# Up projection of a ConvFFN: x's high and low parts side by side, 512 columns in one matmul

## The chip, the cores and the metric

The kernel runs on one core of one Trainium2 chip. The metric is the device time of one execution in microseconds: before the change the median of three timed runs is 317.19 us (317.07 to 317.27). The profile is of one further execution.

## The reference

The input x is 256 tokens of 1024 features in float32. One layer runs (DEPTH = 1), and it is of kind 0: attention in one block of 256 tokens, then a feed-forward part with a causal convolution over three tokens, then a last RMSNorm. Cut to what matters:

```python
hn = _rmsnorm(x, norm_mix[0])
x = x + _moba(hn, w_qkv, w_o)          # 16 heads of 64, plain causal attention at SEQ = 256
x = x + _conv_ffn(_rmsnorm(x, norm_ffn[0]), w_up, conv_w, conv_b, w_down)
return _rmsnorm(x, norm_final)

def _conv_ffn(x, w_up, conv_w, conv_b, w_down):
    u = _causal_dwconv(x @ w_up, conv_w, conv_b)      # 1024 -> 2 * 2816, width 3
    gate, up = jnp.split(u, 2, axis=-1)
    return (jax.nn.silu(gate) * up) @ w_down          # 2816 -> 1024
```

## The kernel before, in words

Precision comes from splitting. Every operand of a matmul is held as a high part (a copy rounded to the reduced float32 type F32R) and a low part (the rest). A product is then three matmuls: high by high, high by low, low by high; `mm3` (lines 227 to 231) writes all products but the first. TensorE takes the first operand of a matmul as the weights it holds, 128 x 128, and streams the columns of the second past them.

For weights, ScalarE makes the high part (`hi_cols`, line 176) and VectorE the low part (`lo_cols`, line 179), each in pieces of 1024 columns. The rows of the trace call such tiles whi and wlo, Vh and Vl, OTh and OTl (the attention's buffers, used again for weights), dhi and dlo (down weights).

x stands transposed, features on partitions: XTh and XTl, each 128 x 8 x 256, high and low part of the normed x without its factor per token. That factor is R (128 x 256, the same in each partition) and is multiplied in after the projection.

The feed-forward part is a loop over 22 chunks c of 128 hidden features (line 660). For each chunk:

- `up(c, 0)` and `up(c, 1)` project the gate half and the up half (g = 0 and 1): for each of 8 steps k over the features, `proj` issues the three matmuls of 128x256 into columns 0 to 255 of one PSUM bank. There are four such banks (psA), so chunk c + 2 takes those of chunk c.
- `scale_r` (line 618) is one VectorE product of the bank with R, into a padded tile (pad00 to pad11, two chunks by two halves).
- `center` (ScalarE, line 622) and two `conv` steps for each half (VectorE, line 627) do the convolution, `sact` (ScalarE, line 692) the silu, `m` (VectorE, line 697) the product of both halves. m is split into mh (ScalarE) and ml (VectorE).
- ScalarE and VectorE also split the down weights of this chunk and the up weights of chunk c + 3 in between.
- `down(c - 2)` adds chunk c - 2's part to the output: 12 matmuls of 128x512, six into the banks of psT and six into psS, which hold the sums over all chunks.

The order on each engine is that in which the code issues; each engine works through its own queue in order and waits by semaphores. Loads come through SyncE's queue as buffers come free. Chunks 0 and 1 are projected while the attention's last part still runs, chunks 2 to 21 in the loop, and chunk 21 has a shorter way of its own (`last_chain`). Behind the loop come the last down matmuls, the last norm and the stores.

Of the kernel before, what the change touches and what calls it, by code (L numbers as in the profile page):

```python
# [8 lines left out]
F32R = mybir.dt.float32r  # L9
BF16 = mybir.dt.bfloat16  # L10
AF = mybir.ActivationFunctionType
# [3 lines left out]
P = 128  # L15
S = 256
D = 1024
KT = D // P
NP = 8
DFF = 2816  # L20
NC = DFF // P
# [29 lines left out]
def hybrid_layer(ctx: ExitStack, tc: tile.TileContext, a):  # L51
    nc = tc.nc
    pe, dve, act, pool = nc.tensor, nc.vector, nc.scalar, nc.gpsimd

    cst = ctx.enter_context(tc.tile_pool(name="cst", bufs=1))
# [8 lines left out]
    def psA():  # L64
        return ps.tile([P, 512], F32, name="psA", tag="A", bufs=4)

    def psS(i):
        return ps.tile([P, 512], F32, name=f"psS{i}", tag=f"S{i}")
# [18 lines left out]
    pads = [[cst.tile([P, S + 2], F32, name=f"pad{i}{g}") for g in range(2)] for i in range(2)]  # L87
# [16 lines left out]
    first = head[:, NPRM:].rearrange("p (i k s) -> p i k s", i=3, k=KT)  # L104
    XTr = first[:, 0]
    x1 = XTr.rearrange("p (t k) s -> p t (k s)", t=2)
    XTh = cst.tile([P, KT, S], F32R, name="XTh")
    XTl = cst.tile([P, KT, S], F32R, name="XTl")
    R = cst.tile([P, S], F32, name="R")
    st = cst.tile([P, 32], F32, name="st")  # L110

# [97 lines left out]
    UP = [Unit(a["wup"][c], 2048, 2) for c in range(NC)]  # L209
# [17 lines left out]
    def mm3(out, l, r, first, last):  # L227
        (lh, ll), (rh, rl) = l, r
        pe.matmul(out, lh, rh, start=first, stop=False)  # L229
        pe.matmul(out, lh, rl, start=False, stop=False)  # L230
        pe.matmul(out, ll, rh, start=False, stop=last)  # L231
# [4 lines left out]
    def gain_lo(k, src, g):  # L236
        dve.scalar_tensor_tensor(XTl[:, k, :], src, g[:, k:k + 1], f32(XTh[:, k, :]),
                                 op0=ALU.mult, op1=ALU.subtract)

    def proj(out, unit, k, off):  # L240
        h, l = unit.v(unit.hi, KT), unit.v(unit.lo, KT)
        mm3(out[:, :S], (h[:, k, off:off + P], l[:, k, off:off + P]), (XTh[:, k, :], XTl[:, k, :]),
            k == 0, k == KT - 1)
# [9 lines left out]
    def bcast_R(c, alloc):  # L253

        rp = alloc()
        for t in range(2):
            pe.transpose(rp[:, t * P:(t + 1) * P], st[:, c + t:c + t + 1].to_broadcast([P, P]), ident)
        act.activation(R, rp[:, :S], AF.Copy)
# [106 lines left out]
    def v_mm(half, part, vp, ts=(0, 1)):  # L365
        u = VW[2 * half + part]
        h, l = u.v(u.hi, 4), u.v(u.lo, 4)
        for t in ts:
            for kk in range(4):
                k = 4 * part + kk  # L370
                tk = slice(t * P, (t + 1) * P)
                mm3(vp[t], (XTh[:, k, tk], XTl[:, k, tk]), (h[:, kk, :], l[:, kk, :]), k == 0, k == KT - 1)
# [24 lines left out]
    for k in range(KT):  # L397
# [4 lines left out]
        c = slice(S * k, S * k + S)  # L402
# [20 lines left out]
    def halves(u, key):  # L423
        return {f"{n}{key}{i}": (lambda f=f, i=i: f(i)) for n, f in (("H", u.split_hi), ("L", u.split_lo)) for i in range(u.n)}

    def scales():
# [3 lines left out]
    start = {"V0": lambda: v_mm(0, 0, vp), "V1": lambda: v_mm(0, 1, vp, (0,)), "V2": lambda: v_mm(0, 1, vp, (1,)),  # L430
             "RS": scales, "BC": lambda: bcast_R(2, lambda: psS(0)), **halves(VW[1], "V"), **halves(QK[2], "Q")}
# [110 lines left out]
    gps = {}  # L542
# [12 lines left out]
    def xsplit(half, ks):  # L555
# [3 lines left out]
        for k in ks:  # L559
            gain_lo(4 * half + k, v[k // 2][:, k % 2, :], g2)  # L560

    def up(c, g, ks):
        if (c, g) not in gps:
            gps[c, g] = psA()
        for k in ks:
            proj(gps[c, g], UP[c], k, g * P)

    for t in range(2):
        wo_mm(5, t, 0)
# [17 lines left out]
    UP[2].split_lo(1)  # L587
    xtr(1, 0)
    up(0, 0, range(4))
    xtr(1, 1)  # L590
    up(0, 1, range(4))
    up(1, 0, range(4))
    xsplit(1, (0, 1))
    xsplit(1, (2, 3))
# [20 lines left out]
    mh, ml = {}, {}  # L615

    def scale_r(c, g):
        dve.tensor_mul(pads[c % 2][g][:, 2:S + 2], gps[c, g][:, :S], R)  # L618

    def center(c, g):  # L620
        y[c, g] = wk.tile([P, S], F32, name=f"y{g}", tag=f"y{g}")
# [38 lines left out]
    for c in range(NC):  # L660
# [5 lines left out]
        if not lone:  # L666
            DN[c].split_hi(0)
        else:
            scale_r(c, 0)
            center(c, 0)  # L670
            DN[c].split_lo(0)
            conv(c, 0, 1)
            conv(c, 0, 0)
        if c > 1:
            up(c, 1, range(KT))
        if lone:
            last_chain(c)
            continue
        scale_r(c, 0)
        scale_r(c, 1)  # L680
        center(c, 0)
        center(c, 1)
# [32 lines left out]


    c0, c1, c2 = NC - 3, NC - 2, NC - 1
    junk = XTl.rearrange("p k s -> p (k s)")
    halves = [slice(0, 512), slice(512, D)]

    def last_add(t, hs, src):
# [94 lines left out]
```

## Time and profile before

| what | value |
|---|---|
| timed runs, median (lowest, highest) | 317.19 us (317.07, 317.27) |
| the profiled execution's own time | 317.43 us |
| its span, first to last instruction | 315.7 us |
| busy TensorE, weight loads | 306.2 us (97%), 281.3 us (89%) |
| busy VectorE, ScalarE, GpSimd | 244.9 us (78%), 202.3 us (64%), 7.2 us (2%) |
| TensorE's share of the chain that ended last | 95% |
| stretch of chunks 5 to 20 | 158.02 to 294.34 us of the span |

The span runs from the first to the last instruction; the execution's own time has 1.7 us more around it. A listed matmul lasts from its start to its modelled end and overlaps the next, so the pace is read from the distance of starts. Engines: PE is TensorE, PEld its weight loads, DVE VectorE, ACT ScalarE. In a row of the order of time, what stands in brackets is the idle time of the engine before it and who ended it.

### The profile page before, as it was taken

The page shows a single profiled execution, that of the slowest core. Times are in us where ns is not written, and L with a number is a line of the kernel's source. Part 1 is how long each engine was busy: PE and PEld are TensorE (multiplying, and loading weights), DVE is VectorE, ACT ScalarE, POOL GpSimd, SP SyncE. Part 2 cuts the span into 40 slices and gives each one's busy share as a digit, 9 for nine tenths or more (in the row PEclk, how much of TensorE's full clock was granted, in tenths as well). Part 3 has the DMA queues.
Part 4 walks back from the last instruction along what each step waited for, and adds up shares of the span by engine and source line. Part 5 has one row for each costly group of instructions (what it writes and reads, how often), then busy time and mean ns, then how long its engine had stood idle before and what let it go on. Part 6 is the DMA issues. An engine that isn't in the chain of part 4 may idle for free.

```text
span 315.7 us, 5386 instructions
## 1 busy us (share of the span) xinstructions
PE 306.2 (97%) x2067; PEld 281.3 (89%) x2067; DVE 244.9 (78%) x482; ACT 202.3 (64%) x369; POOL 7.2 (2%) x25
## 2 busy tenths in 40 slices
PE   7999999999999999999999999999999999999990
PEld 5988899988998889999999999999999999999980
DVE  4866888887999957499997778887777777774784
ACT  5975878877989726667785566656556556553323
POOL 4000000000000000000000000000000000000001
PEclk9999999999999999999999999999999999999996
DMA  7997442763050694348666454445565511210003
GB/s 239 383 415 320 163 191 92 296 247 135 8 185 10 244 419 173 98 154 313 212 265 253 159 172 163 197 183 199 202 199 190 180 38 61 69 66 0 2 1 133
DMA packets 13897, 55.49 MB, mean 176 GB/s; under 512 B 1328, under 2 KB 4656, under 8 KB 10160
## 3 DMA queue, kind: packets, MB, share of 16 engines
q1 hardware_dynamic: 13168, 54.24, 46.9%
q10 hardware_dynamic: 704, 0.92, 1.0%
q8 instruction: 16, 0.26, 0.3%
q14 instruction: 9, 0.07, 0.1%
HBM read 54.10 MB, written 1.05 MB: 175 GB/s over the span
## 4 chain that ended last, share of the span: by engine, by line
PE 95%; DVE 1%; DMA 1%; issue 1%; ACT 1%; DVEq 0%; ACTq 0%
PE psA L231 21%; PE psA L230 21%; PE psA L229 21%; PE psS L230 4%; PE psS L231 4%; PE psT L231 4%; PE psT L230 4%; PE psS L229 4%; PE psT L229 4%; PE psT L335 2%; PE psA L410 1%; PE psA L412 1%; PE psA L414 1%; DMA head<-in_first 1%; DVE x_sb L728 0%
## 5 line engine op out<-in xcount | busy, mean ns | idle before, releaser
L231 PE MATMUL psA<-XTh,wlo 128*128 128x256 f32 x288 | 81.6, 283 | 0.0
L230 PE MATMUL psA<-XTl,whi 128*128 128x256 f32 x288 | 81.5, 283 | 0.0
L229 PE MATMUL psA<-XTh,whi 128*128 128x256 f32 x288 | 81.3, 282 | 0.0
L229 PEld LDWEIGHTS psA<-XTh,whi 128*128 128x128 f32 x288 | 54.5, 189 | 0.7
L230 PEld LDWEIGHTS psA<-XTl,whi 128*128 128x128 f32 x288 | 54.2, 188 | 0.7
L231 PEld LDWEIGHTS psA<-XTh,wlo 128*128 128x128 f32 x288 | 54.3, 189 | 0.0
L622 ACT ACTIVATE y<-pad,head 128x256 f32<-128x256 f32 x43 | 25.3, 600 | 40.8 <-DVE pad L618 40.8
L618 DVE TENSOR_TENSOR pad<-psA,R 128x256 f32<-128x256 f32 x43 | 17.7, 420 | 38.3 <-PE psA L231 34.6
L179 DVE TENSOR_TENSOR wlo<-head,whi 128x1024 fp32r<-128x1024 f32 (+1 forms) x48 | 44.8, 951 | 2.4 <-ACT whi L176 2.3
L176 ACT ACTIVATE whi<-head 128x1024 fp32r<-128x1024 f32 (+1 forms) x48 | 38.8, 833 | 1.7 <-DMA head<-in_first 1.6
L627 DVE SCALAR_TENSOR_TENSOR y<-pad,head,y 128x256 f32<-128x256 f32 x86 | 36.1, 478 | 1.3 <-ACT y L622 1.3
L179 DVE TENSOR_TENSOR dlo<-rawd,dhi 128x1024 fp32r<-128x1024 f32 x29 | 35.3, 1216 | 0.1
L176 ACT ACTIVATE dhi<-rawd 128x1024 fp32r<-128x1024 f32 x29 | 30.2, 1048 | 2.6 <-PE psA L231 2.1
L231 PE MATMUL psA<-XTh,OTl 128*128 128x256 f32 x80 | 22.8, 285 | 0.0
L231 PE MATMUL psA<-XTh,Vl 128*128 128x256 f32 x80 | 22.7, 284 | 0.0
L230 PE MATMUL psA<-XTl,OTh 128*128 128x256 f32 x80 | 22.7, 284 | 0.0
L230 PE MATMUL psA<-XTl,Vh 128*128 128x256 f32 x80 | 22.7, 283 | 0.0
L229 PE MATMUL psA<-XTh,Vh 128*128 128x256 f32 x80 | 22.5, 281 | 0.0
L229 PE MATMUL psA<-XTh,OTh 128*128 128x256 f32 x80 | 22.5, 281 | 0.0
L692 ACT ACTIVATE sact<-y 128x256 f32<-128x256 f32 x21 | 8.8, 418 | 16.4 <-DVE y L627 16.4
L231 PE MATMUL psT<-dhi,ml 128*128 128x512 f32 x42 | 16.7, 397 | 0.0
L230 PE MATMUL psT<-dlo,mh 128*128 128x512 f32 x42 | 16.6, 395 | 0.0
(176 smaller groups left out, 680.0 us busy)
## 6 DMA issues: line engine op xcount, KB each, us to landing
head<-in_wup SPq DMA_DIRECT2D x12, 1024.0 KB, 4.9
rawd<-in_wdn SPq DMA_DIRECT2D x22, 512.0 KB, 3.3
raw<-in_wup SPq DMA_DIRECT2D x10, 1024.0 KB, 4.8
raw<-in_wqk SPq DMA_DIRECT2D x4, 1024.0 KB, 7.5
rawd<-in_wo SPq DMA_DIRECT2D x8, 512.0 KB, 3.3
head<-in_first SPq DMA_DIRECT2D x7, 384.0 KB, 6.6
raw<-in_wv SPq DMA_DIRECT2D x4, 512.0 KB, 8.8
head<-in_wv SPq DMA_DIRECT2D x2, 1024.0 KB, 4.9
```

Of the source, the lines that this page charges most:

```text
L176: act.activation(self.hi[:, c], self.raw[:, c], AF.Copy)
L179: dve.tensor_sub(self.lo[:, c], self.raw[:, c], f32(self.hi[:, c]))
L229: pe.matmul(out, lh, rh, start=first, stop=False)
L230: pe.matmul(out, lh, rl, start=False, stop=False)
L231: pe.matmul(out, ll, rh, start=False, stop=last)
L335: pe.transpose(PT[j][:, h, b * P:(b + 1) * P], PR[j][:, h, b * P:(b + 1) * P], ident)
L410: pe.matmul(o[:, :S], u.v(u.hi, KT)[:, k, off:off + P], XTh[:, k, :], start=k == 0, stop=False)
L412: pe.matmul(o[:, :S], u.v(u.hi, KT)[:, k, off:off + P], XTl[:, k, :], start=False, stop=False)
L618: dve.tensor_mul(pads[c % 2][g][:, 2:S + 2], gps[c, g][:, :S], R)
L622: act.activation(y[c, g], pads[c % 2][g][:, 2:S + 2], AF.Identity, scale=cw[:, 2, g * NC + c:g * NC + c + 1], bias=cb[:, g * NC + c:g * NC ...
L627: dve.scalar_tensor_tensor(y[c, g], pads[c % 2][g][:, j:j + S], cw[:, j, col:col + 1], y[c, g], op0=ALU.mult, op1=ALU.add)
L692: act.activation(sact, y[c, 0], AF.Silu)
```

## The change

XTh and XTl become two views of one tile XT of 128 x 8 x 2 x 256, so that for each k the high and the low part lie side by side as 512 columns. In chunks 5 to 20 (`wide`) each step k is two matmuls: the high weights with all 512 columns, so that the bank's left half gets high by high and its right half high by low, and the low weights with the 256 high columns, into the left half. The bank's two halves are then summed: ScalarE copies the right half into the padded tile, VectorE adds the left half to it and multiplies by R in a further step. Chunks 0 to 4 and 21 stay as they were. The scratch target of the last norm's squares (junk) is now the whole of XT.

```diff
-    XTh = cst.tile([P, KT, S], F32R, name="XTh")
-    XTl = cst.tile([P, KT, S], F32R, name="XTl")
+    XT = cst.tile([P, KT, 2, S], F32R, name="XT")
+    XTh, XTl = XT[:, :, 0, :], XT[:, :, 1, :]
...
+    def wide(c):
+        return 5 <= c < NC - 1
+
+
     def up(c, g, ks):
         if (c, g) not in gps:
             gps[c, g] = psA()
         for k in ks:
-            proj(gps[c, g], UP[c], k, g * P)
+            if not wide(c):
+                proj(gps[c, g], UP[c], k, g * P)
+                continue
+            h, l = (UP[c].v(t, KT)[:, k, g * P:(g + 1) * P] for t in (UP[c].hi, UP[c].lo))
+            pe.matmul(gps[c, g], h, XT[:, k], start=k == 0, stop=False)
+            pe.matmul(gps[c, g][:, :S], l, XTh[:, k, :], start=False, stop=k == KT - 1)
...
     def scale_r(c, g):
-        dve.tensor_mul(pads[c % 2][g][:, 2:S + 2], gps[c, g][:, :S], R)
+        u, v = pads[c % 2][g][:, 2:S + 2], gps[c, g]
+        if wide(c):
+            act.activation(u, v[:, S:], AF.Copy)
+            dve.tensor_add(u, v[:, :S], u)
+            dve.tensor_mul(u, u, R)
+        else:
+            dve.tensor_mul(u, v[:, :S], R)
...
-    junk = XTl.rearrange("p k s -> p (k s)")
+    junk = XT.rearrange("p k i s -> p (k i s)")
```

TensorE at the start of chunk 8's up projection, behind the last down matmuls of chunk 5, before (psS_1693 is an output bank; XTh and XTl the parts of x; whi and wlo the chunk's up weights):

```order
L230 MATMUL psS_1693<-dlo,mh 128x512
L231 MATMUL psS_1693<-dhi,ml 128x512
L229 MATMUL psA<-XTh,whi 128x256
L230 MATMUL psA<-XTl,whi 128x256
L231 MATMUL psA<-XTh,wlo 128x256
L229 MATMUL psA<-XTh,whi 128x256
L230 MATMUL psA<-XTl,whi 128x256
L231 MATMUL psA<-XTh,wlo 128x256
```

And now at the same place:

```order
L230 MATMUL psS_1692<-dlo,mh 128x512
L231 MATMUL psS_1692<-dhi,ml 128x512
L574 MATMUL psA<-XT,whi 128x512
L575 MATMUL psA<-XT,wlo 128x256
L574 MATMUL psA<-XT,whi 128x512
L575 MATMUL psA<-XT,wlo 128x256
```

Two matmuls stand where three stood, 32 in a chunk for 48; the down matmuls around them are as before.

VectorE in chunk 8, from the first product with R, before (pad_82 and pad_83 are the padded tiles of gate and up half, y the convolved tiles):

```order
L618 TENSOR_TENSOR pad_82<-psA,R 128x256
L618 TENSOR_TENSOR pad_83<-psA,R 128x256
L179 TENSOR_TENSOR dlo<-rawd,dhi 128x1024
L627 SCALAR_TENSOR_TENSOR y_2222<-pad_82,head,y_2222 128x256
L627 SCALAR_TENSOR_TENSOR y_2224<-pad_83,head,y_2224 128x256
```

And now:

```order
L630 TENSOR_TENSOR pad_82<-psA,pad_82 128x256
L631 TENSOR_TENSOR pad_82<-pad_82,R 128x256
L630 TENSOR_TENSOR pad_83<-psA,pad_83 128x256
L631 TENSOR_TENSOR pad_83<-pad_83,R 128x256
L179 TENSOR_TENSOR dlo<-rawd,dhi 128x1024
```

Two products became two adds, each with its product behind it; the rest of the chunk stands in the same order.

ScalarE in chunk 8, from the split of the chunk's down weights, before:

```order
L176 ACTIVATE dhi<-rawd 128x1024
L622 ACTIVATE y_2222<-pad_82,head 128x256
L622 ACTIVATE y_2224<-pad_83,head 128x256
L176 ACTIVATE OTh<-raw_127 128x1024
L692 ACTIVATE sact<-y_2222 128x256
```

And now:

```order
L176 ACTIVATE dhi<-rawd 128x1024
L629 ACTIVATE pad_82<-psA 128x256
L629 ACTIVATE pad_83<-psA 128x256
L637 ACTIVATE y_2173<-pad_82,head 128x256
L637 ACTIVATE y_2175<-pad_83,head 128x256
L176 ACTIVATE OTh<-raw_126 128x1024
L707 ACTIVATE sact<-y_2173 128x256
```

Both copies stand between the split of the down weights and the first bias step, so that step is now behind the copy of the second half as well.

## Rows read from the trace of the kernel before

**Rows 1.** The page: TensorE's part of the engine totals (busy us, share of the span, instructions), and the shares of the chain that ended last, by engine and by line.

```profile
PE 306.2 (97%) x2067; PEld 281.3 (89%) x2067; DVE 244.9 (78%) x482; ACT 202.3 (64%) x369; POOL 7.2 (2%) x25
...
PE 95%; DVE 1%; DMA 1%; issue 1%; ACT 1%; DVEq 0%; ACTq 0%
PE psA L231 21%; PE psA L230 21%; PE psA L229 21%; PE psS L230 4%; PE psS L231 4%; PE psT L231 4%; PE psT L230 4%; PE psS L229 4%; PE psT L229 4%; PE psT L335 2%; PE psA L410 1%; PE psA L412 1%; PE psA L414 1%; DMA head<-in_first 1%; DVE x_sb L728 0%
```

**Rows 2.** The table of windows, for the stretch from chunk 5's first up matmul to chunk 21's: length, then busy us and instructions of PE, PEld, DVE, ACT and POOL, granted clock, DMA share, GB/s.

```profile
158.02:294.34 136.32, 136.32 (x962) 128.12 (x960) 102.18 (x178) 77.49 (x113) 0.00 (x0) 1.00 0.42 150
```

**Rows 3.** TensorE in order of time around chunk 8's up block: start us, length us, engine, line, operation, out<-in, shape. The down block begins at 180.81, its second half at 182.21, the up block at 183.58, the next down block at 189.33, chunk 9's up block at 192.10.

```profile
180.81 0.39 PE L229 MATMUL psT<-dhi,mh 128*128 128x512 f32 x1
...
182.21 0.39 PE L229 MATMUL psS<-dhi,mh 128*128 128x512 f32 x1
182.43 0.40 PE L230 MATMUL psS<-dlo,mh 128*128 128x512 f32 x1
...
183.58 0.28 PE L229 MATMUL psA<-XTh,whi 128*128 128x256 f32 x1
183.69 0.28 PE L230 MATMUL psA<-XTl,whi 128*128 128x256 f32 x1
183.81 0.28 PE L231 MATMUL psA<-XTh,wlo 128*128 128x256 f32 x1
183.93 0.28 PE L229 MATMUL psA<-XTh,whi 128*128 128x256 f32 x1
...
189.33 0.39 PE L229 MATMUL psT<-dhi,mh 128*128 128x512 f32 x1
189.57 0.40 PE L230 MATMUL psT<-dlo,mh 128*128 128x512 f32 x1
...
192.10 0.28 PE L229 MATMUL psA<-XTh,whi 128*128 128x256 f32 x1
```

**Rows 4.** TensorE in order of time, first matmul of a K projection (24 of them) and the matmul behind its last.

```profile
40.84 0.28 PE L229 MATMUL psA<-XTh,whi 128*128 128x256 f32 x1
...
43.69 0.39 PE L229 MATMUL psA<-pth,Vh 128*128 128x512 f32 x1
```

**Rows 5.** Weight loads in order of time, the two behind the border at 183.58.

```profile
183.58 0.19 PEld L230 LDWEIGHTS psA<-XTl,whi 128*128 128x128 f32 x1
183.70 0.19 PEld L231 LDWEIGHTS psA<-XTh,wlo 128*128 128x128 f32 x1
```

**Rows 6.** Groups by line and form, over the span: line, engine, operation, out<-in, shapes, count | busy us, mean ns of one | idle time before.

```profile
L618 DVE TENSOR_TENSOR pad<-psA,R 128x256 f32<-128x256 f32 x43 | 17.7, 420 | 38.3 <-PE psA L231 34.6 <-ACT R L258 3.7
...
L697 DVE TENSOR_TENSOR m<-sact,y 128x256 f32<-128x256 f32 x21 | 8.8, 419 | 0.5 <-ACT sact L692 0.3
...
L272 ACT ACTIVATE QH<-psA 128x256 fp32r<-128x256 f32 x8 | 2.9, 364 | 1.0 <-PE psA L414 1.0
```

**Rows 7.** VectorE in order of time: the products with R of chunks 2, 3 and 5, then chunk 8 from the end of chunk 7's work, to chunk 9's products.

```profile
143.98 0.75 DVE L618 TENSOR_TENSOR pad<-psA,R 128x256 f32<-128x256 f32 x2
...
150.30 0.75 DVE L618 TENSOR_TENSOR pad<-psA,R 128x256 f32<-128x256 f32 x2
...
162.95 0.42 DVE L618 TENSOR_TENSOR pad<-psA,R 128x256 f32<-128x256 f32 x1
...
186.68 0.41 DVE L703 TENSOR_TENSOR ml<-m,mh 128x256 fp32r<-128x256 f32 x1
187.02 0.41 DVE L618 TENSOR_TENSOR pad<-psA,R 128x256 f32<-128x256 f32 x1
189.53 0.42 DVE L618 TENSOR_TENSOR pad<-psA,R 128x256 f32<-128x256 f32 x1 [2.10 <-PE psA L231]
...
195.20 0.42 DVE L703 TENSOR_TENSOR ml<-m,mh 128x256 fp32r<-128x256 f32 x1
195.53 0.42 DVE L618 TENSOR_TENSOR pad<-psA,R 128x256 f32<-128x256 f32 x1
198.05 0.43 DVE L618 TENSOR_TENSOR pad<-psA,R 128x256 f32<-128x256 f32 x1 [2.10 <-PE psA L231]
```

**Rows 8.** ScalarE in order of time: the split of chunk 5's down weights, behind the scaling of the last norm's gains (fold); chunk 8's second bias step; the split of chunk 9's down weights.

```profile
162.97 1.04 ACT L176 ACTIVATE dhi<-rawd 128x1024 fp32r<-128x1024 f32 x1
...
189.99 0.60 ACT L622 ACTIVATE y<-pad,head 128x256 f32<-128x256 f32 x1 [1.87 <-DVE pad L618]
...
194.50 1.05 ACT L176 ACTIVATE dhi<-rawd 128x1024 fp32r<-128x1024 f32 x1
```

**Rows 9.** VectorE in order of time near the end: chunk 21's first product with R, and two steps of its last chain, the second of which reads what the first wrote.

```profile
297.41 0.42 DVE L618 TENSOR_TENSOR pad<-psA,R 128x256 f32<-128x256 f32 x1 [1.06 <-PE psA L231]
...
301.85 0.29 DVE L656 TENSOR_TENSOR m<-sact,y 128x128 f32<-128x128 f32 x1
302.18 0.23 DVE L657 CAST mh<-m 128x128 fp32r<-128x128 f32 x1
```

**Rows 10.** TensorE in order of time: chunk 7's first up matmul, and the first down matmul of chunk 8.

```profile
175.06 0.28 PE L229 MATMUL psA<-XTh,OTh 128*128 128x256 f32 x1
...
206.37 0.39 PE L229 MATMUL psT<-dhi,mh 128*128 128x512 f32 x1
```

## The prediction

> **What bounds the kernel now.** I read four things in this order: engine totals and the chain of waits on the page, TensorE's order of time over one chunk of the feed-forward loop, the other two engines over the same chunk, and last how far they run ahead. The page gives TensorE 97% of the span and 95% of the chain, shared by three lines of one helper [rows 1]. From chunk 5's first up matmul to chunk 21's (158.02 to 294.34 us) the table of windows shows it busy for all of 136.32 us at a granted clock of 1.00, the upper of its two levels, while VectorE has 102.18 and ScalarE 77.49 us [rows 2]. That is 8.52 us a chunk, the distance of the first up matmuls of chunks 8 and 9 [rows 3]. Nothing TensorE needs is late in the loop, so what counts is the distance between starts of its matmuls, not their listed durations of 0.28 and 0.39 us, which overlap.
>
> That distance comes from counts. Chunk 8's 48 up matmuls of 256 columns run from 183.58 to 189.33: 5.75/48 = 119.8 ns each. The 12 down matmuls of 512 columns ahead of them run from 180.81 to 183.58: 2.77/12 = 230.8 ns [rows 3]. Two of 256 thus take 239.6, one of 512 takes 230.8: each matmul carries something like 9 ns whatever its width, and the rest goes with the columns.
>
> **The change part by part.** *Matmuls.* In 16 chunks, for 2 halves and 8 steps of k (256 places), three matmuls of 256 columns become one of 512 and one of 256. The columns stay 768. Out goes 3 x 119.8 = 359.4 ns, in comes 230.8 + 119.8 = 350.6 ns: 8.8 ns less, 2.25 us in all. The trace has no place where the widths alternate over and over, only borders: the first 256 behind a 512 takes 0.11 us to the next start (183.58 to 183.69), the first 512 behind a 256 takes 0.24 (189.33 to 189.57) [rows 3]. Their sum, 0.35 us, agrees, with a slight lean to the shorter side of the 256. I take 10 ns per place, 2.6 us.
>
> Both sides of that: within the down block the six matmuls into psT take 1.40/6 = 233.3 ns and the six into psS 1.37/6 = 228.3 [rows 3]; a K projection of 24 matmuls of 256 takes 2.85/24 = 118.8 [rows 4]. The pair then lies between 347.1 and 353.1 ns and the gain between 6.3 and 12.3 ns, 1.6 to 3.1 us. Taking single border steps as if they repeated (512: 0.22 to 0.24; 256: 0.11 to 0.13 with rounding) would widen this to 0.33 to 0.37 us, from 7.5 us gained to 2.7 us lost; those are steps of single rows, rounded to 10 ns, and I keep them for the outer ends only.
>
> The Trainium skill (page "TensorE: Matmul & The Clock Gate", section "Back-to-back issue gap") speaks against this change: it gives the distance of warm matmuls as columns over 2.4 GHz and about 2.5 ns, so that fixed cost would be 2.5 ns and the gain an estimated 0.6 us. This case's rows differ: 119.8 and 230.8 ns stand well above the 109 and 216 ns of that rule, so the measured difference goes into the sum and the rule stands among the rivals.
>
> *Weight loads.* One of three goes, since the high weights are loaded once for both parts of x. The next load starts with the running matmul (183.58 for both) [rows 3, 5], so loads lie beside matmuls. No term of its own; whatever they add is within the 119.8 and 230.8.
>
> *Sum of the halves.* Per chunk ScalarE gets two PSUM copies; the like of it, 128x256 out of PSUM, takes 364 ns [rows 6]. VectorE gets two more operations: instead of one PSUM product (420 ns) an add that reads PSUM and a product in SBUF, whose like takes 419 [rows 6]. Back to back VectorE steps start 0.33 apart (187.02 behind 186.68), but a step that needs the one before it waits for its full length: at the end of the kernel a 0.29 us product is followed 0.33 us later by the step that reads it [rows 7, 9]. An add costs its 0.42 and 0.04, the product behind it 0.34. VectorE's own cycle, read where it does not wait (143.98 to 150.30), is 6.32 us [rows 7]. Less two products (0.67), plus 2 x 0.80: 7.25 us. TensorE's new chunk is 8.52 - 16 x 0.010 = 8.36. So VectorE keeps 1.1 us, where it now waits 2.10 us a chunk for the second half [rows 7]. That idle time pays for the change.
>
> *What queues behind the new waits.* ScalarE's copies wait for TensorE; behind them stand the two bias steps, the split of the weights three chunks ahead and the silu. Those waited before too, for VectorE's products of the same banks (1.87 us at 189.99) [rows 8], so they start later by copy, add and product less the old product: 0.36 + 0.46 + 0.42 - 0.42, some 0.8 us. Who waits for them? The split low parts and the low part of m. Chunk 8's low m part ends at 195.62 and its down matmuls start at 206.37 [rows 7, 10], so 10.7 us lie between. The PSUM bank of (5, 0) is read at 162.95, that of chunk 7 behind it is needed at 175.06 [rows 7, 10]. A delay of 0.8 us reaches nobody; nor does chunk 5's, where the first copy stands behind a split that ends at 164.01 and VectorE, free at 162.95, waits 1.06 and the copy's 0.46, 1.5 us [rows 7, 8]. Chunk 20's tail, which lacks later splits, has VectorE waiting 1.06 us in front of chunk 21's first product [rows 9]; 0.9 us more fits. Should it not, the overhang of a few tenths stands at the end.
>
> *Layout.* One tile in place of two, with the same bytes; every row ahead of chunk 5 is the same. Cost nothing, and no instruction there to carry one.
>
> Sum: 317.43 (the profiled execution, span 315.7 and 1.7 around it) - 2.6 = 314.8. That execution stands 0.24 above the median, so the timed runs should come to 314.6 us. With the narrow bounds 314.0 to 315.6.
>
> **Rivals.** *No gain from the width (no change).* If in the alternation every 512 goes at its border value behind a 256, 0.24, and the 256 at 119.8, the pair costs 359.8 ns against 359.4: 317.2 to 317.3 us; with a third of the 8.8 ns it is 316.5. For it: each 512 now does follow a 256. Against it: the twelve of a down block bear that border step too and still average 230.8. Chance 0.10. The rule of the page "TensorE: Matmul & The Clock Gate" named above would land here as well, at an estimated 316.6; 0.03 of the chance is for it, since its level is not this trace's.
>
> *A larger gain.* If loading weights holds up narrow matmuls and the 512 hides a load, the 256 goes at 0.11, its border value: 230.8 + 110 = 340.8 ns, 18.6 ns x 256 = 4.8 us, 312.4 us. For it: 183.58 to 183.69. Against: the next load starts only with the 256 itself, so it is no better hidden than now. Chance 0.09.
>
> *The evacuation becomes the bound (slower).* Place: copy, add, product, in the cycle VectorE to ScalarE. If each add waits its copy in full (2 x 0.46) and copies stand behind the 1.05 us split of the down weights [rows 8], VectorE's 7.25 grow to 9.2 us. The lag over 16 chunks is then 16 x (9.2 - 8.36) = 13.4 us; 10.7 of it is covered by the lead and the rest, 2.7, eats the gain. This is the point from which it decides. With the 0.60 us bias step exposed as well it is 9.8: 23.0 - 10.7 = 12.3 us lost, 2.6 gained, 327 us. Against it: the split is done before the second half ends (194.50 against 198.05 in the next chunk) [rows 7, 8], so these waits do not add up. Chance 0.04.
>
> *Alternating widths cost more than either stream (slower).* With 0.24 and 0.13 at each place: 0.37, 10.6 ns lost, 320 us. Chance 0.03. That the change does something else than it says I leave out: the order shows 32 matmuls for 48 in each chunk.
>
> **How the numbers follow.** Forecast 0.74, no gain 0.10, larger gain 0.09, slower 0.07. A measurement here tells 0.2%, 0.63 us, from no change. Faster by more: 0.74 + 0.09 and a little from the no-gain edge, 0.84; within: 0.09; slower: 0.07. The range holds the forecast with its bounds and the larger gain: 312.2 to 316.4.
>
> **What would show it.** Right: starts of the wide and narrow matmul of one k some 0.35 us apart in pairs, chunks 8.36 us apart, TensorE without a gap, and VectorE's wait ahead of its second bank below 2.1 us, now for ScalarE. Wrong: pairs at 0.36 (no gain), 0.34 (larger), or gaps on TensorE ahead of a chunk's first up or down matmul whose releaser is VectorE, growing from chunk to chunk (evacuation).

## The result and the profile after

The changed kernel takes 314.98 us (median of 5 runs, 314.62 to 316.23), the kernel before 317.19 us in the same comparison (5 runs, 317.01 to 317.51). The ratio is 0.9936 with a 95% interval of 0.9923 to 0.9948: faster by 0.6%, or 2.2 us. The forecast was 314.6 us with a range of 312.2 to 316.4.

The profiled execution took 315.09 us, its span 313.3. The page's engine totals (busy us, share of the span, instructions) and the shares of its chain, to set beside [rows 1]:

```profile
PE 303.8 (97%) x1811; PEld 268.0 (86%) x1811; DVE 259.6 (83%) x514; ACT 211.3 (67%) x401; POOL 7.2 (2%) x25
...
PE 95%; DVE 1%; DMA 1%; issue 1%; ACT 1%; DVEq 0%; ACTq 0%
```

256 matmuls and 256 weight loads are gone, and VectorE and ScalarE have 32 instructions more each. TensorE still makes 95% of the chain, so nothing has taken its place. The table of windows shows the same for the stretch from chunk 5's first up matmul to chunk 21's; columns as in [rows 2]:

```profile
158.32:291.97 133.65, 133.65 (x705) 114.59 (x704) 116.06 (x208) 86.50 (x145) 0.00 (x0) 1.00 0.44 153
```

The stretch is 133.65 us long where it was 136.32 [rows 2], 2.67 us less, and TensorE is busy for all of it at the same granted clock of 1.00. Behind it 313.3 - 291.97 = 21.3 us are left; before, 315.7 - 294.34 = 21.4. Chunk 5 starts 0.30 us later than before, although every instruction ahead of it is the same; in the profiles of the nine experiments that leave the work ahead of it alone, that start lies anywhere from 157.33 to 159.79. So the gain is in the loop, and the head adds scatter.

TensorE in order of time around chunk 8's up block (start, length, engine, line, operation, shape), to set beside [rows 3]:

```profile
183.38 0.40 PE L574 MATMUL psA<-XT,whi 128*128 128x512 f32 x1
183.62 0.27 PE L575 MATMUL psA<-XT,wlo 128*128 128x256 f32 x1
183.73 0.39 PE L574 MATMUL psA<-XT,whi 128*128 128x512 f32 x1
...
188.98 0.40 PE L229 MATMUL psT<-dhi,mh 128*128 128x512 f32 x1
...
191.73 0.40 PE L574 MATMUL psA<-XT,whi 128*128 128x512 f32 x1
```

The lengths (0.40 and 0.27) overlap; the starts count. A wide and a narrow matmul together take 0.35 us (183.38 to 183.73). The 16 pairs run from 183.38 to 188.98, 5.60/16 = 350 ns, in place of three at 119.8. The block is 5.60 us long instead of 5.75, and chunks 8 and 9 stand 8.35 us apart instead of 8.52.

What the sum of the halves costs the other engines is seen on VectorE and ScalarE. VectorE, in order of time: the first adds of chunks 5 and 6, then chunk 8, then the step ahead of chunk 21's first product, and that product:

```profile
164.62 0.42 DVE L630 TENSOR_TENSOR pad<-psA,pad 128x256 f32<-128x256 f32 x1 [1.27 <-ACT pad L629]
...
172.19 0.42 DVE L630 TENSOR_TENSOR pad<-psA,pad 128x256 f32<-128x256 f32 x1 [0.23 <-ACT pad L629]
...
188.08 0.42 DVE L630 TENSOR_TENSOR pad<-psA,pad 128x256 f32<-128x256 f32 x1 [0.23 <-ACT pad L629]
...
189.66 0.42 DVE L630 TENSOR_TENSOR pad<-psA,pad 128x256 f32<-128x256 f32 x1 [0.69 <-ACT pad L629]
...
294.51 0.42 DVE L718 TENSOR_TENSOR ml<-m,mh 128x256 fp32r<-128x256 f32 x1 [0.48 <-ACT mh L715]
295.05 0.42 DVE L633 TENSOR_TENSOR pad<-psA,R 128x256 f32<-128x256 f32 x1
```

And ScalarE in chunk 8:

```profile
187.69 0.36 ACT L629 ACTIVATE pad<-psA 128x256 f32<-128x256 f32 x1
189.24 0.38 ACT L629 ACTIVATE pad<-psA 128x256 f32<-128x256 f32 x1 [1.19 <-PE psA L575]
```

The 2.10 us for which VectorE waited for the second bank [rows 7] have become 0.23 + 0.69 = 0.92 us of waiting for copies, and ScalarE waits for TensorE in its place (1.19). In front of chunk 21's first product VectorE waited 1.06 us for TensorE [rows 9]; at 295.05 it does not wait for it any more, so the room that was there is used up, and no more than that. The view of waits over the whole span (engine, line and what it waited for: us in total, times, longest) has these as the largest new entries, and none in which TensorE waits for line 629, 630 or 631:

```profile
ACT pad L629 <- PE psA L575: 17.9, 15, 2.1
...
DVE pad L630 <- ACT pad L629: 15.9, 30, 1.6
```

### The profile page after: what moved, and what is told of

It is laid out like the page before. It is cut to its first block, busy times and chain, and to the rows that moved or that the text cites. A ratio compares the mean times of both kernels' runs of the same rounds, so it can differ in the third digit from the quotient of the medians.

```text
span 313.3 us, 4955 instructions
## 1 busy us (share of the span) xinstructions
PE 303.8 (97%) x1811; PEld 268.0 (86%) x1811; DVE 259.6 (83%) x514; ACT 211.3 (67%) x401; POOL 7.2 (2%) x25
## 4 chain that ended last, share of the span: by engine, by line
PE 95%; DVE 1%; DMA 1%; issue 1%; ACT 1%; DVEq 0%; ACTq 0%
PE psA L574 19%; PE psA L231 11%; PE psA L230 11%; PE psA L229 11%; PE psA L575 10%; PE psS L230 4%; PE psS L231 4%; PE psT L231 4%; PE psT L230 4%; PE psT L229 4%; PE psS L229 4%; PE psT L335 2%; PE psA L410 2%; PE psA L412 1%; PE psA L414 1%; DMA head<-in_first 1%
## 5 line engine op out<-in xcount | busy, mean ns | idle before, releaser
L229 PE MATMUL psA<-XT,whi 128*128 128x256 f32 x160 | 45.4, 284 | 0.0
L230 PE MATMUL psA<-XT,whi 128*128 128x256 f32 x160 | 45.2, 282 | 0.0
L231 PE MATMUL psA<-XT,wlo 128*128 128x256 f32 x160 | 45.2, 282 | 0.0
L574 PE MATMUL psA<-XT,whi 128*128 128x512 f32 x128 | 45.1, 393 | 0.0
L575 PE MATMUL psA<-XT,wlo 128*128 128x256 f32 x128 | 36.0, 282 | 0.0
L229 PEld LDWEIGHTS psA<-XT,whi 128*128 128x128 f32 x160 | 30.2, 189 | 0.4
L230 PEld LDWEIGHTS psA<-XT,whi 128*128 128x128 f32 x160 | 30.1, 188 | 0.4
L231 PEld LDWEIGHTS psA<-XT,wlo 128*128 128x128 f32 x160 | 30.2, 189 | 0.0
L574 PEld LDWEIGHTS psA<-XT,whi 128*128 128x128 f32 x128 | 24.0, 188 | 5.5
L630 DVE TENSOR_TENSOR pad<-psA,pad 128x256 f32<-128x256 f32 x32 | 13.6, 424 | 15.9 <-ACT pad L629 15.9
L575 PEld LDWEIGHTS psA<-XT,wlo 128*128 128x128 f32 x128 | 24.1, 188 | 0.3
L629 ACT ACTIVATE pad<-psA 128x256 f32<-128x256 f32 x32 | 11.9, 374 | 17.9 <-PE psA L575 17.9
L574 PE MATMUL psA<-XT,OTh 128*128 128x512 f32 x64 | 22.6, 393 | 0.0
L574 PE MATMUL psA<-XT,Vh 128*128 128x512 f32 x64 | 22.6, 393 | 0.0
L707 ACT ACTIVATE sact<-y 128x256 f32<-128x256 f32 x21 | 8.8, 418 | 16.4 <-DVE y L642 16.4
L575 PE MATMUL psA<-XT,Vl 128*128 128x256 f32 x64 | 18.0, 282 | 0.0
```

Of the source, the lines that this page charges most:

```text
L574: pe.matmul(gps[c, g], h, XT[:, k], start=k == 0, stop=False)
L575: pe.matmul(gps[c, g][:, :S], l, XTh[:, k, :], start=False, stop=k == KT - 1)
L629: act.activation(u, v[:, S:], AF.Copy)
L630: dve.tensor_add(u, v[:, :S], u)
L707: act.activation(sact, y[c, 0], AF.Silu)
```

## The experiments

Each batch has its own runs of the kernel before; those scatter more in the later batches (median 317.31 in the first, 318.72 and 318.41 in the others, with lows of 316.75, 316.75 and 317.28 us), so there I read the loop's length in the trace beside the ratio.

### The layout alone

```diff
 def wide(c):
-    return 5 <= c < NC - 1
+    return False
```

> Layout alone: one tile XT, but no chunk is wide, so all matmuls and the evacuation are those of before. My theory (the layout costs nothing, the 0.3 us by which chunk 5 starts later in the changed kernel's profile is scatter of the start): 317.2 us, chunks 5 to 20 in 136.3 us. Rival (the layout itself costs 0.3 us at the start): 317.5 us, chunk 5 starting at 158.3 us again.

Measured: 317.75 us (12 runs), ratio 1.0004 (0.9986 to 1.0022). The same stretch of windows:

```profile
159.04:295.36 136.32, 136.32 (x961) 128.12 (x960) 102.21 (x178) 77.48 (x113) 0.00 (x0) 1.00 0.44 151
```

136.32 us, to the last digit that of the kernel before. One tile in place of two costs nothing in the loop. At the start, chunk 5 begins at 159.04, within the scatter named above, so a cost of some tenths there would not be seen; the interval of the ratio leaves room for 0.2%.

### The sum of the halves alone, without the wide matmul

```diff
-            pe.matmul(gps[c, g], h, XT[:, k], start=k == 0, stop=False)
+            pe.matmul(gps[c, g][:, :S], h, XTh[:, k, :], start=k == 0, stop=False)
+            pe.matmul(gps[c, g][:, S:], h, XTl[:, k, :], start=False, stop=False)
```

> Evacuation alone: the bank's two halves are filled and summed as in the changed kernel, but with three matmuls of 256 columns per step. Theory (the evacuation is hidden, all of the gain is the width): 317.2 us, chunk distance 8.52 us. Rival (the evacuation costs something that the width paid for): above 317.7 us, with gaps on TensorE. Second rival (the gain comes from writing the two products to different halves, not from the width): 315.0 us.

Measured: 317.41 us (12 runs), ratio 1.0004 (0.9984 to 1.0024). Its windows:

```profile
157.49:293.81 136.32, 136.32 (x961) 128.12 (x960) 116.24 (x208) 86.47 (x145) 0.00 (x0) 1.00 0.43 150
```

VectorE has its 116 us and ScalarE its 86, as in the changed kernel, and the loop is the old one. So the copies, adds and products are hidden entirely, writing the two products to different halves gains nothing, and the whole gain is that one wide matmul stands for two narrow ones. With the second narrow matmul goes its weight load too, since every matmul in these traces has one; no run takes away the one without the other.

### Eight wide, then eight narrow

```diff
+        for k in ks:
+            if wide(c):
+                l = UP[c].v(UP[c].lo, KT)[:, k, g * P:(g + 1) * P]
+                pe.matmul(gps[c, g][:, :S], l, XTh[:, k, :], start=False, stop=k == KT - 1)
```

The narrow matmul leaves the first loop over k and gets this one of its own.

> The changed kernel with the matmuls of a half grouped: first its eight of 512 columns, then its eight of 256. Theory (each matmul has its own cost, no matter what stands beside it): 315.0 us, a half in 8 x 230.5 + 8 x 119.3 = 2.80 us. Rival (the alternation itself helps, because the 512 hides the next load): up to 317 us. Rival (the alternation costs): below 314.6 us.

Measured: 314.01 us (4 runs), ratio 0.9880 (0.9834 to 0.9925). TensorE in order of time, the first half of chunk 8's up block and the start of the second (rows of eight):

```profile
182.37 2.02 PE L574 MATMUL psA<-XT,whi 128*128 128x512 f32 x8
184.23 1.12 PE L578 MATMUL psA<-XT,wlo 128*128 128x256 f32 x8
185.18 2.02 PE L574 MATMUL psA<-XT,whi 128*128 128x512 f32 x8
```

Eight wide take 1.86 us (232.5 ns each), eight narrow 0.95 (118.8). The loop is 133.55 us, against 133.65 with alternating widths: the order of the widths is worth at most 0.1 us. The rivals that gave alternation a price or a gain of its own fall. The median's lead over the changed kernel is no evidence: in this profile the loop starts at 157.33.

### Each up matmul cut in two of 128 columns

An edit of the kernel before, for chunks 5 to 20:

```diff
+            for i, (w, x) in enumerate(((h, XTh), (h, XTl), (l, XTh))):
+                for t in range(2):
+                    n = slice(t * P, (t + 1) * P)
+                    pe.matmul(gps[c, g][:, n], w, x[:, k, n], ...
```

> The kernel before, with each up matmul of 256 columns in chunks 5 to 20 cut into two of 128 with the same weights. Theory (a matmul costs some 9 ns besides its columns, whatever its width): a 128 takes 64 ns, each of 256 places 26 ns more, 324 us. Rival (the distance of narrow matmuls is that of their weight loads, which start 0.12 us apart): 110 to 120 ns for a 128, some 84 us more, about 400 us.

Measured: 396.54 us (4 runs), ratio 1.2505 (1.2468 to 1.2543). TensorE in order of time, chunk 8's first up matmuls and the one behind its last:

```profile
198.31 0.33 PE L573 MATMUL psA<-XTh,whi 128*128 128x128 f32 x2
...
208.97 0.45 PE L229 MATMUL psT<-dhi,mh 128*128 128x512 f32 x1
```

96 matmuls in 10.66 us, 111 ns each: half the columns of a 119.8 ns matmul, and almost all of its time. With 16 x 96 x 111 ns = 170.5 us in place of 16 x 48 x 119.8 = 92.0 the difference is 78.5 us, and 79.2 were measured. A cost of 9 ns for each of the 16 x 48 matmuls that were added would have given some 7 us. So what a matmul carries beside its columns is not one amount. That the weight load sets the distance of the narrow ones is shown by the next run. The Trainium skill (page "TensorE: Matmul & The Clock Gate", section "LDWEIGHTS (loading the stationary operand)") puts a load at its 128 columns over 1.2 GHz, an estimated 107 ns; the 111 ns here agree.

### The narrow matmul on 128 of its 256 columns

```diff
-            pe.matmul(gps[c, g][:, :S], l, XTh[:, k, :], start=False, stop=k == KT - 1)
+            pe.matmul(gps[c, g][:, :P], l, XTh[:, k, :P], start=False, stop=k == KT - 1)
```

This leaves out half of the product of the low weights and high x.

> The changed kernel with the low weights applied to the first 128 of x's 256 high columns only (half of that product is left out). Theory 1 (a matmul costs its columns and some 9 ns): the narrow one falls from 119 to 64 ns, 55 ns x 256 less, 301 us. Theory 2 (the next load starts with the running matmul and takes some 112 ns, so no matmul is shorter than that, behind a 512 neither): it falls to 112, 2 us less, 313 us.

Measured: 313.59 us (2 runs, 312.47 and 314.71), ratio 0.9856 (0.9811 to 0.9901); loop 159.79 to 291.63, 131.84 us. TensorE in order of time in chunk 8:

```profile
185.08 0.22 PE L575 MATMUL psA<-XT,wlo 128*128 128x128 f32 x1
185.14 0.45 PE L574 MATMUL psA<-XT,whi 128*128 128x512 f32 x1
185.42 0.22 PE L575 MATMUL psA<-XT,wlo 128*128 128x128 f32 x1
```

And its weight loads there:

```profile
185.08 0.19 PEld L574 LDWEIGHTS psA<-XT,whi 128*128 128x128 f32 x1
185.19 0.19 PEld L575 LDWEIGHTS psA<-XT,wlo 128*128 128x128 f32 x1
```

The pair takes 185.42 - 185.08 = 0.34 us. 128 columns fewer save (133.65 - 131.84)/256 = 7 ns a place. The wide matmul starts 0.06 us behind the narrow one, so two starts can be closer than 0.11. The loads are not: that of the wide matmul begins at 185.08, with the narrow one and no earlier, the next at 185.19, 0.11 behind it, when the wide matmul has already begun; and the next narrow one comes 0.28 behind the wide one, in place of 0.23. So it is the loads that keep the pair at 0.11 + 0.23. A wide matmul ahead does not hide the load that the narrow one has to cover. That was the condition of the rival with the larger gain, and it is not met.

### The wide matmul on 384 columns

```diff
-            pe.matmul(gps[c, g], h, XT[:, k], ...
+            pe.matmul(gps[c, g][:, :384], h, XT[:, k].rearrange(...)[:, :384], ...
...
-            act.activation(u, v[:, S:], AF.Copy)
+            act.activation(u, v[:, P:384], AF.Copy)
```

This leaves out half of the product of the high weights and low x, and ScalarE copies columns 128 to 383 in place of the right half; only the time is of use.

> The changed kernel with the wide matmul over 384 columns instead of 512 (half of high weights by low x is left out). Both theories (above 112 ns the columns set the distance, with some 9 ns beside them): the wide one falls from 230.5 to 175 ns, 14.2 us less, 301 us. Rival (the matmul of 512 has a loss of its own that one of 384 does not have): below 170 ns, under 299.5 us.

Measured: 303.53 us (2 runs), ratio 0.9539 (0.9505 to 0.9574). TensorE in order of time, chunk 8's up block, and the end of the loop:

```profile
187.15 0.34 PE L574 MATMUL psA<-XT,whi 128*128 128x384 f32 x1
187.33 0.28 PE L575 MATMUL psA<-XT,wlo 128*128 128x256 f32 x1
187.44 0.34 PE L574 MATMUL psA<-XT,whi 128*128 128x384 f32 x1
...
191.75 0.39 PE L229 MATMUL psT<-dhi,mh 128*128 128x512 f32 x1
...
283.54 0.40 PE L231 MATMUL psT<-dhi,ml 128*128 128x512 f32 x1
287.50 0.76 PE L757 MATMUL psT<-whi,mh 128*128 128x512 f32 x1 [3.57 <-DVE mh L672]
...
290.62 0.41 PE L230 MATMUL psS<-dlo,mh 128*128 128x512 f32 x1
```

The pair takes 4.60/16 = 287.5 ns; with 118 to 119 for the narrow one, which is taken from the other runs, 384 columns take an estimated 169 ns. With the other widths: 111 for 128, 119 for 256, 169 for 384, 230 for 512. From 256 to 384 the step is 50 ns and from 384 to 512 it is 61; the time is no straight line in the columns. What makes it bend is not shown.

The same run shows a second thing. Its loop (157.84 to 275.07) is 117.23 us, 16.4 less than 133.65, but the whole kernel is only 11.4 us faster than 314.98. VectorE's cycle, 7.57 us there, is above TensorE's 7.33, so it falls 16 x 0.24 = 3.8 us behind; TensorE has no gap in the loop, and pays behind it. From 283.54 to 287.50 lie 3.96 us where 0.23 is usual, 3.7 us lost to the wait for VectorE. The seven matmuls from 287.50 to 290.62 then take 3.12 us where 7 x 0.23 = 1.6 is usual, at a granted clock of 0.50, the lower level: 1.5 us more. Both together are about the missing 5 us.

### Four and eight more VectorE products in each chunk

```diff
             dve.tensor_mul(u, u, R)
+            for _ in range(2):
+                dve.tensor_mul(x_sb[:, 0, :S], R, R)
```

Four in a chunk, since this runs for each half; with range(4) eight. They write a scratch that nobody reads at that point.

> The changed kernel with four further products of 128x256 on VectorE in each wide chunk (they write scratch, nothing reads them). VectorE's cycle grows from 7.4 to some 8.8 us, over TensorE's 8.35. Theory (10.7 us of lead between the low part of m and its down matmuls): the lag grows by 0.4 us a chunk, 7 us in all, and reaches nobody: 315.0 us. Rival (TensorE is fed with less lead than that): up to 322 us, with gaps on TensorE from the first wide chunks on.

> The same with eight further products: VectorE's cycle some 10.1 us, 1.75 over TensorE's. Theory: the lag passes the lead of 10.7 us after six chunks, then TensorE follows VectorE's cycle: some 15 us more, 330 us, first gap on TensorE in chunk 11 or 12. Rival (less lead): the first gap some chunks earlier and up to 340 us. Rival (VectorE is not what the sums come through): 315 us.

Measured: 328.01 us with four (4 runs; ratio 1.0328, 1.0268 to 1.0387), 359.69 with eight (4 runs; 1.1304, 1.1244 to 1.1363). With four, VectorE in order of time, the first add of two chunks that follow each other:

```profile
246.49 0.43 DVE L630 TENSOR_TENSOR pad<-psA,pad 128x256 f32<-128x256 f32 x1 [0.23 <-ACT pad L629]
...
255.65 0.43 DVE L630 TENSOR_TENSOR pad<-psA,pad 128x256 f32<-128x256 f32 x1 [0.23 <-ACT pad L629]
```

Its cycle is 9.16 us, 0.81 above TensorE's 8.35. TensorE in order of time:

```profile
264.64 0.50 PE L231 MATMUL psT<-dhi,ml 128*128 128x512 f32 x1 [0.28 <-DVE ml L720]
...
307.55 0.80 PE L229 MATMUL psT<-dhi,mh 128*128 128x512 f32 x1 [5.70 <-ACT mh L717]
308.14 0.63 PE L230 MATMUL psT<-dlo,mh 128*128 128x512 f32 x1
308.57 0.63 PE L231 MATMUL psT<-dhi,ml 128*128 128x512 f32 x1
...
312.77 0.47 PE L759 MATMUL psT<-whi,mh 128*128 128x512 f32 x1 [2.30 <-DVE mh L674]
```

Up to chunk 17's up block TensorE shows no gap: the lead I had read, 10.7 us, is there. The first wait for VectorE stands behind that block, at 264.64. Yet the kernel is 13.0 us slower than the changed one, where I had expected no cost. VectorE's first add of chunk 5 and its first product of chunk 21 show the lag:

```profile
164.01 0.42 DVE L630 TENSOR_TENSOR pad<-psA,pad 128x256 f32<-128x256 f32 x1 [1.28 <-ACT pad L629]
...
307.87 0.42 DVE L635 TENSOR_TENSOR pad<-psA,R 128x256 f32<-128x256 f32 x1
```

They are 143.86 us apart, in the changed kernel 295.05 - 164.62 = 130.43: 13.4 us of lag, near the 16 x 0.81 = 13.0 of the cycles. From that product to the end of the span it is 325.9 - 307.87 = 18.0 us here and 313.3 - 295.05 = 18.3 there. So all of the lag is paid. What the lead hid comes due at the end, where nothing is left to run ahead with. Windows of this kernel for that end:

```profile
307.50:313.00 5.50, 3.15 (x7) 2.08 (x8) 4.97 (x13) 1.90 (x3) 0.00 (x0) 0.66 0.00 0
```

The granted clock is 0.66 there, a mean over stretches at both levels: behind the idle time of 5.70 us the 512-column matmuls start 0.43 us apart (308.14, 308.57), about twice 230 ns, which is the lower level, 1.2 GHz. Here that cost nothing: TensorE waits another 2.30 us for VectorE right behind them (312.77).

With eight the cycle is 11.0 us, not the 10.1 I had assumed, since a product that overwrites what the one before it wrote starts a full length behind it, 0.46 us, and any other 0.34. With eight, six of them are of the first kind: 7.57 + 6 x 0.46 + 2 x 0.34 = 11.0; with four, two: 7.57 + 2 x 0.46 + 2 x 0.34 = 9.17. The 7.57 us are the changed kernel's cycle while VectorE catches up (first adds at 164.62 and 172.19). (11.0 - 8.35) x 16 = 42 us of lag; 44.7 more than 314.98 were measured, where the lead had made me expect about 330 us. The view of waits shows the weight loads of the down matmuls waiting for ScalarE's high part of m, which waits for VectorE's m:

```profile
PEld psT L229 <- ACT mh L717: 28.6, 13, 8.8
```

### Two more products

One in place of the loop of two, so that the cycle ends just below TensorE's.

> The changed kernel with two further products on VectorE in each wide chunk. From the runs with four and eight (chunk distances 9.17 and 11.0 us) a product costs 0.46 us and VectorE's own cycle is 7.35: with two it is 8.26 us, just under TensorE's 8.35. Theory (only a cycle above TensorE's costs anything, and then all of it): 315.0 us. Rival (the lead is eaten by any delay): 0.9 us a chunk, up to 329 us.

Measured: 314.58 us (4 runs), ratio 0.9883 (0.9852 to 0.9913). Windows:

```profile
158.15:291.80 133.65, 133.65 (x706) 114.57 (x704) 125.63 (x239) 87.18 (x145) 0.00 (x0) 1.00 0.44 153
```

VectorE in order of time, the first adds of chunks 15 and 16:

```profile
246.89 0.42 DVE L630 TENSOR_TENSOR pad<-psA,pad 128x256 f32<-128x256 f32 x1 [0.23 <-ACT pad L629]
...
255.13 0.43 DVE L630 TENSOR_TENSOR pad<-psA,pad 128x256 f32<-128x256 f32 x1 [0.23 <-ACT pad L629]
```

VectorE works 9.6 us more and the loop is 133.65 us again. A cycle of 8.24 us (the wait of 0.23 us for a copy included) is free, one of 9.16 costs its whole excess. That I had expected 8.26 is luck: a product alone adds 0.34 and not 0.46 us, and the cycle without it is 7.57 and not 7.35.

### The change from chunk 0 on, and from chunk 2 on

```diff
 def wide(c):
-    return 5 <= c < NC - 1
+    return c < NC - 1
```

> Chunks 0 to 20 wide instead of 5 to 20. Theory (each wide chunk saves 16 x 10.4 ns = 0.17 us and VectorE's lag reaches nobody): 0.8 us below the changed kernel, 314.2 us. Rival (in chunks 2 to 5 VectorE has no idle time, so 0.9 us more a chunk delays it until TensorE waits for a bank): 315.0 us or more, with gaps on TensorE ahead of up or down matmuls between 130 and 165 us.

Measured: 315.24 us (6 runs), ratio 0.9925 (0.9906 to 0.9944). Five more chunks should have given 5 x 0.167 = 0.8 us; nothing came. TensorE in order of time behind chunk 2's up block:

```profile
138.03 0.39 PE L229 MATMUL psT<-dhi,mh 128*128 128x512 f32 x1
139.38 0.50 PE L230 MATMUL psT<-dlo,mh 128*128 128x512 f32 x1 [0.96 <-DVE dlo L179]
```

1.35 us lie between two starts that are 0.23 apart elsewhere: 1.1 us lost, more than the 0.8 gained. TensorE waits for the low part of chunk 0's down weights, which VectorE makes from 138.11 on, and VectorE is late from chunk 0's first add on:

```profile
130.65 0.43 DVE L630 TENSOR_TENSOR pad<-psA,pad 128x256 f32<-128x256 f32 x1 [5.47 <-ACT pad L629]
...
138.11 1.22 DVE L179 TENSOR_TENSOR dlo<-rawd,dhi 128x1024 fp32r<-128x1024 f32 x1
```

ScalarE shows what the copy for that add stands behind:

```profile
129.28 1.06 ACT L176 ACTIVATE dhi<-rawd 128x1024 fp32r<-128x1024 f32 x1 [0.50 <-issue]
130.25 0.64 ACT L629 ACTIVATE pad<-psA 128x256 f32<-128x256 f32 x2
```

The copies stand behind the split of the down weights in ScalarE's order. But most of the 5.47 us is no new wait. VectorE at the same place in the changed kernel, where chunk 0 is narrow:

```profile
129.17 0.76 DVE L633 TENSOR_TENSOR pad<-psA,R 128x256 f32<-128x256 f32 x2 [3.80 <-ACT R L258]
131.24 1.77 DVE L642 SCALAR_TENSOR_TENSOR y<-pad,head,y 128x256 f32<-128x256 f32 x4 [1.31 <-ACT y L637]
```

There it waits 3.80 us for R and 1.31 behind the same split, 5.11 together; in this run the 5.47 are followed by 0.28, together 5.75. So 0.6 us of waiting is new. The two adds and two products stand for two products and take 1.60 us (130.65 to 132.25) in place of some 0.67, which is 0.9 us more. So the rival's result came, and for the larger part by its reason, the added work of a VectorE with nothing to spare; at chunk 0 there is no lead yet that would cover either. Whether copies ahead of that split would keep the gain was not tried.

With 2 for 0 in the same line:

> Chunks 2 to 20 wide: the two chunks whose longer evacuation stood ahead of the first down weights' low part in the run from chunk 0 stay narrow. Theory (that stall was the whole price of starting earlier): no gap on TensorE behind chunk 2, 3 x 0.17 = 0.5 us below the changed kernel, 314.5 us. Rival (VectorE without idle time in chunks 2 to 5 delays later down matmuls too): a gap of 0.5 us or more between 140 and 165 us, 315.0 us or more.

Measured: 314.43 us (6 runs), ratio 0.9883 (0.9861 to 0.9905). There is no such wait on TensorE, and from chunk 2's first up matmul (132.31) to chunk 21's (291.00) it takes 158.69 us; the changed kernel takes 159.14 (132.83 to 291.97), the kernel before 161.81 (132.53 to 294.34). Three more chunks give 0.45 us where 3 x 0.167 = 0.5 was due. This version is faster than the kernel before; against the changed kernel the loop shows the 0.45 us, while the two medians, from different batches, cannot tell so little.

## Why the prediction was right, and where it was not

**Matmuls: right.** I took 10 ns for each of 256 places, 2.6 us. The loop lost 2.67 us, 10.4 ns a place: some 2.4 us in the up blocks (16 x 0.15), the rest in rounding and in the down blocks (2.75 us for 2.77). The pair was put at 350.6 ns and took 350. That it came from one wide matmul in place of two narrow ones is shown by the run that has all the rest of the change and no gain.

**The reason given for it: only half right.** "Each matmul carries something like 9 ns whatever its width" falls. Two widths gave a line, and two more show that it is none: from 128 to 256 columns a matmul takes 8 ns more, from 256 to 384 an estimated 50, from 384 to 512 an estimated 61. At 128 the weight load of 111 ns rules; why the last two steps differ is not shown. The sum was right because it used the measured distances of exactly the two widths at stake, not the line through them.

**The rule that spoke against it.** The loop's gain came out at 2.67 us. By the Trainium skill (page "TensorE: Matmul & The Clock Gate", section "Back-to-back issue gap"), whose formula of columns over 2.4 GHz and 2.5 ns the section gives for an isolated matmul, it would have been an estimated 0.6 us. For streams of a load and a matmul each, the same section of the Trainium skill gives about 81 ns at 128 columns and 131 at 512; here it is 111 and 230, and the measurement decides. The Trainium skill says there too that loads enter the distance at small widths, which the runs with 128 columns bear out.

**Weight loads: right as far as it goes.** They were given no term, and the sum needed none. Loads can follow each other at 0.11 us, and at 256 and 512 columns the matmuls are further apart than that. Whether a part of what a matmul costs beside its columns at 256 is its load's no run separates, so the 10 ns of a place may be a matmul's or its load's.

**Sum of the halves: right that it is hidden, VectorE's cycle put too short.** VectorE was to keep 1.1 us idle in a chunk and waits 0.92; the second copy takes 0.38 instead of 0.36 us and starts when the bank is done. But 0.23 of the 0.92 is not to spare. The first copy stands behind ScalarE's split of the down weights, so the first add waits for it in every chunk, also where VectorE is the slower engine (the runs with more products). The sum left this wait out, and an add behind a wait starts a full length behind the step before it and not 0.33 us: 7.25 + 0.23 + 0.09 = 7.57 us, the distance of the first adds of chunks 5 and 6. TensorE's chunk of 8.35 leaves 0.78 us. The prediction has that split only in a rival, and argued there that it does not add up. Chunk 5's first add was to wait 1.5 us and waited 1.27, which reached nobody. Chunk 20's tail was to use up most of VectorE's 1.06 us in front of chunk 21's first product. It used up all of it, with no cost behind it: the part behind the loop is 21.3 us, and was 21.4.

**Layout: right** for the loop, shown by the run with the layout alone; at the start it is not seen above the scatter.

**The rival in which the evacuation becomes the bound: its mechanism is real, its point was wrong.** I let the lead of 10.7 us cover the lag, so that a cycle of 9.2 us would cost 13.4 - 10.7 = 2.7 us. The run with four more products had a cycle of 9.16 us and paid 13.0. The step that failed is "10.7 of it is covered by the lead": the lead only moves the wait to the end. The rival decides from a cycle of 8.35 us, not from 9.2. The changed kernel's VectorE needs 7.57 us, so it was right not to give this rival more, but its margin is 8.35 - 7.57 = 0.78 us a chunk, where the prediction had 1.1 us and the lead on top of it.

**The last 0.4 us.** 314.98 is 0.4 above the forecast. The loop gave slightly more than forecast. In the two profiled executions the difference lies in where the loop starts (158.32 against 158.02), which scatters by 2.5 us over profiles with the same instructions ahead; so how close the total came is in part luck, and the 2.67 us of the loop are what bears the forecast out.

## What to carry to other kernels

Where two matmuls use the same weights, putting their columns side by side saves the difference between the measured distances, here 10 ns at 256 columns, and more at 128, where a matmul takes the 111 ns of its weight load and two of them an estimated 222, while one of 256 takes 119. Measure the distances at the very widths in question. Before work is moved to another engine, compare that engine's cycle with the bound engine's cycle: up to equality it is free, beyond it costs the excess times the number of rounds, and a lead hides that until the end and no longer. Look at the first rounds by themselves: before any lead exists, added work and added waits reach the bound engine, and two chunks too early gave the gain back here. Count as the cycle also the waits that stay when the engine is the slower one: here 0.23 us of what looked like idle time was such a wait.

## What was not expected of the hardware

- 128 columns take 111 ns and 256 take 119: half the work at almost the same price. Loads hold that distance: two matmuls started 0.06 us apart, two loads never under 0.11 in the rows shown.
- 384 columns take an estimated 169 ns, so the last 128 of 512 cost 61 ns and the 128 before them 50. The cause stays open.
- Idle time of TensorE near the end can be paid for twice, since the matmuls right behind it run at the lower clock level: with 384 columns seven of them cost 1.5 us beside the 3.7 us of the wait. With four more products the same clock (0.43 us apart in place of 0.23) cost nothing, as TensorE had to wait again behind them.
